# A hybrid decoder layer on one core: rows of the mixed activations and of h loaded in larger pieces into other buffers, and one PSUM bank fewer in rotation

## The chip, the cores and the metric

The kernel runs on one core of a Trainium2 chip. The metric is the device time of one execution, in microseconds (us); the time before is the median of three executions, 2020.22 us (2017.64 to 2026.35). A profiled execution is a further one, taken with the hardware profiler. The engines are named as in the profile: PE (matrix products; PEld its weight loads), ACT (activations and copies), DVE (elementwise), POOL (elementwise, slower), SP (here used to issue DMAs). SPq and ACTq are the DMA issues of SP and ACT.

## The reference

One layer over 2048 tokens of width 1024, all in float32:

```python
hn = rms_norm(h, mix_pre_g)
proj = hn @ w_in                                  # q, k, v and the conv group's input u
attn_out = sliding_window_attention(q, k, v, attn_sinks, rel_bias)
conv_out = conformer_conv(u, conv_dw, conv_dw_b, conv_ln_g, conv_ln_b, w_conv_pw)
mixed = jnp.concatenate([attn_out, conv_out], axis=-1) @ w_out
h = h + rms_norm(mixed, mix_post_g)
hn = rms_norm(h, ffn_pre_g)
ff = (jax.nn.silu(hn @ w_gate) * (hn @ w_up)) @ w_down
h = h + rms_norm(ff, ffn_post_g)
```

The attention has 8 heads of width 64 and a window of 128; the convolution group is a GLU, a causal depthwise convolution of 31 taps, a layer norm, a swish and a 512 by 512 product. The feed-forward width is 2816.

## The kernel before, in words

**Numbers.** Every float32 operand of a product is split into a high and a low part (a copy by ACT, then a subtraction by DVE or POOL), and each product is three matmuls, high by high, high by low, low by high. A split operand is a tile `hl(tag)` of 128 partitions by 2 by 512. The tokens are cut into four blocks of T = 512; the channels into eight blocks (c or k) of 128.

**Stages**, by the label that the names in the profile carry after the @:

- A0 to A3: the input projection of the four token blocks. Its last four channel blocks are the queries.
- B0 to B3: attention. Each of four sub-blocks writes its 128 tokens into `mixT[0:4]`, a DRAM buffer of eight channel blocks by 2048 tokens, from a tile `at` (L517 to L522).
- C0 to C3: the convolution. The taps run on DVE beside the products of other stages (L554). The tail (L568) turns the sums in the PSUM bank `ct` into a tile `yt`, takes the norm, turns them back and writes `mixT[4:8]` (L607).
- U: the pointwise product and the lower half of `w_out` are multiplied once into `fold`.
- W0 to W3: the output projection of the four token blocks (`stage_w`, L693), with its norm (`norm_w`, L745), which writes h into `h_scr` and the normed h into `hn_scr`.
- H0, H2: the operands of the feed-forward for the first pair of token blocks (0 and 1) and the second (2 and 3). `stage_h_plain` (L822) loads columns of `hn_scr`, turns four 128 by 128 pieces on PE, has ACT copy them out scaled (L828), sends that to `hT` and splits it. `stage_h_sums` (L835) forms sums and differences from `hT` and the other block's columns, two blocks of channels at a step, four steps, three tiles `chl` each.
- F0, F2: gate and up products of a pair, in a scheme that needs seven products where eight would be plain (`STEPS`, L867). A part is computed early (`stage_pre`, L880) and kept in DRAM (`keeps`); the rest is `stage_p1` (L950).
- G0, G2: the down projection of a pair, again seven types of products (`stage_p2`, L1108). `finish` (L1086) norms the result, loads rows of h from `h_scr`, adds them and writes `out`. In G0 it runs four times, with two jobs of 128 rows each: O0.1 and O0.3 after type 5, E0.1 and E0.3 after type 6.

**`stage_w` in more detail.** W0 takes the eight channel blocks in four groups of two, W1 to W3 in two groups of four. For a group, `acts` (L699) loads the rows of `mixT` one channel block at a time into a tile with the tag `mtag` (`fa` for W0, `at` for the others) and splits each into a tile `hl(htags[gi])`. Then, for the two halves n of the output, the weights are loaded and four chains of matmuls follow, one for each 128 tokens. The next group's `acts` is called before the second half (L728). In W1 the second group's `acts` is called in the middle of the eight early products of F0 that stand between the groups (L733 to L738). The chains of W2 and W3 go to the PSUM banks `tr`, and the results to four tiles `mid`.

**Buffers.** A tile is asked for by tag, and each tag has a fixed number of buffers, which its tiles share:

```python
BUFS = dict(x=4, p=4, wx=1, gb=2, hl=8, ql=4, chl=5, mid=4, mb=2, fa=4, at=2, fc=3, glu=2, yt=1, raw=2, w=6)
mm = lambda: bank("mm", 4)
tr = lambda: bank("tr", 3)
ct = lambda: bank("ct", 1)
```

`wx`, `chl` and `raw` hold two blocks of 512 columns, `yt` four. `chl` is used by U, by A1, by the splits of W1 to W3 (second group), by `norm_w` (one tile of gains and four of x), by the sums of H and by the weights of F. `wx` is used at the start, by U, by the sums of `w_down` (`stage_tsums`, L1070) and by the rows of h in G0.

**What sets the order.** The program is traced as one main line of stages (`run`, L1343) and several lanes of side work (`Lane`, L1265), which are pumped by the main line's progress: lane `lw` holds in this order C2, W2, C3, W3, the first half of H2, and W3's norm, and runs beside G0; lane `lf` holds the four calls of `finish`; lane `lh` the sums of H. The context that places the instructions (L1491) lays them out on the engines by a simulated timeline, with the traced order as their priority; each engine then runs its own list in order and waits where data or a buffer isn't there.

Of the kernel before, what the change touches and what calls it, by code (L numbers as in the profile page):

```python
# [12 lines left out]
F32 = mybir.dt.float32  # L13
# [4 lines left out]
AF = mybir.ActivationFunctionType  # L18
ALU = mybir.AluOpType
# [6 lines left out]
P = 128  # L26
T = 512
# [10 lines left out]
def layer_kernel(ctx, tc, x, xT, cols, rows, sinks, relb, onehot, w_in, w_pw, w_out, w_gate, w_up, w_down, out):  # L38
    nc = tc.nc
# [15 lines left out]
    def t_(tag, shape, dt=F32):  # L55
        return sb.tile(list(shape), dt, tag=tag, name=nm(tag), bufs=BUFS[tag])

    def f4(tag, shape=(P, D)):
        return t_(tag, shape)

    def f2(tag, shape=(P, T)):
        return t_(tag, shape)

    def hl(tag):
        return t_(tag, (P, 2, T), F32R)
# [624 lines left out]
                vtt(acc[i][:, cs], acc[i][:, cs], o, ALU.add)  # L690
            yield 0.65 * len(units)

    def stage_w(w, atag, htags, mtag, bank_of, norm=None, ready=None):  # L693
        G = KC // len(htags)
        L = f"W{w}"
        lab[0] = L
        acc = [f4(atag) for _ in range(4)]

        def acts(gi):  # L699
            aa = []  # L700
            lab[0] = L
            for c in range(G * gi, G * gi + G):
                m = f2(mtag)
                nc.sync.dma_start(m, mixT[c, :, w * T : (w + 1) * T])
                a = hl(htags[gi])
                act(a[:, 0], m, AF.Copy)
                vtt(a[:, 1], m, a[:, 0].bitcast(F32), ALU.subtract)
                aa.append([a])
            return aa

        def weights(gi, n):
            ws = []
            for c in range(G * gi, G * gi + G, 2):
                if c < 4:
                    ws += weight(w_out[c : c + 2, :, n * T : (n + 1) * T].rearrange("c p t -> p c t"), lo_out[n, c : c + 2], w > 0, on_pool=False)
                else:
                    for j in range(2):
                        ws.append(hl("w"))
                        nc.sync.dma_start(ws[-1].bitcast(F32), fold[n, c - 4 + j])
            return ws  # L720

        nxt = acts(0)
        yield W_LEAD
        for gi in range(KC // G):
            aa = nxt
            for n in range(2):
                lab[0] = L
                if n == 1 and gi + 1 < KC // G and not (ready and G * gi + G == 4):  # L728
                    nxt = acts(gi + 1)
                ws = weights(gi, n)  # L730
                yield from block_half(acc, list(zip(aa, ws)), n, gi == 0, L, bank_of)
            if ready and G * gi + G == 4:
                for i, c in enumerate(ready()):  # L733
                    if i == Q0 // 2:
                        ld.until("C1")
                        lab[0] = L
                        nxt = acts(gi + 1)
                    yield c  # L738
        tail = norm_w(w, acc)
        if norm:  # L740
            norm(tail)
        else:
            yield from tail
# [60 lines left out]
    def turned(w, k, bank_of, tag):  # L804
        c = load_cols(w, k, tag)
        b = bank_of()
        for s in range(4):
            nc.tensor.transpose(b[:, s * P : (s + 1) * P], c[:, s], ident)
        return b
# [12 lines left out]
    def stage_h_plain(ws, ops, n, off):  # L822
        L = f"H{ws[0]}"
        for k in range(4):
            lab[0] = L
            b = turned(ws[0], k + off, tr if ws[0] else ct, COLTAG[ws[0]][k] if ws[0] else "fa")
            u = f2("gb")
            act(u, b, AF.Copy, scale=g_ffn[:, k + off : k + off + 1])  # L828
            nc.scalar.dma_start(hT[ws[0] // 2][k + off], u)
            o = op_tile(ws, ops, n, k, {})  # L830
            act(o[:, 0], u, AF.Copy)
            lo(u, o, False)
            yield 2.0
# [46 lines left out]
    def stage_pre(ws, ops, mid, keep, q0=0, q1=None):  # L880
        PRE = PRES[ws[0]]
        q1 = q1 or 2 * PRE
        L = f"F{ws[0]}"
        raws = {}
        wops = {}
        kept = {}

        def load(q):
            if q < q1 and q % 2 == 0:
                lab[0] = L  # L890
                half, m = divmod(q, PRE)
                raw = t_("raw", (P, 2, T))
                for j in range(2):
                    src, pr = MATS[m + j]
                    nc.sync.dma_start(raw[:, j], src[2 * pr][:, half * T : (half + 1) * T])
                    raws[q + j] = raw[:, j]

        def fetch(q):
            if PRE <= q < q1:
                lab[0] = L  # L900
                kept[q] = f2("gb")
                nc.sync.dma_start(kept[q], keep[q - PRE])

        def split(q):
            if q < q1:
                lab[0] = L
                raw = raws.pop(q)
                wops[q] = split_f(raw, hl("w"))
                lo(raw, wops[q], ws[0] and q % 2 == 1)

        seeded = {}

        def seed(q):
            if PRE <= q < q1:
                lab[0] = L
                seeded[q] = mm()
                act(seeded[q], kept.pop(q), AF.Copy)  # L917

        load(q0)
        load(q0 + 2)  # L920
        for q in range(q0, q0 + 3):
            split(q)
        for q in range(q0, q1):
            half, m = divmod(q, PRE)
            started.add(f"P{ws[0]}.{q}")
            bn = "B21" if half else "B11"
            if len(ops.get(bn, ())) < 4:
                lh.until(f"{bn}.{ws[0]}")
            split(q + 3)
            load(q + 4)  # L930
            fetch(q + 2)
            lab[0] = L
            seed(q + 1)
            lab[0] = L
            o = seeded.pop(q) if half else mm()
            product(o, wops.pop(q), ops[bn], not half)
            if not half:
                u = f2("fa")
                act(u, o, AF.Copy)
                nc.scalar.dma_start(keep[m], u)  # L940
            else:
                if MATS[m][0] is w_gate:
                    sg = f2("fa")
                    act(sg, o, AF.Silu)
                else:
                    vtt(sg, sg, o, ALU.mult)
                    nc.sync.dma_start(mid[0, MATS[m][1]], sg)
            yield 2.76
# [137 lines left out]
    def finish(L, gb, jobs, pool=True):  # L1086
        lab[0] = L
        n_ = len(jobs)
        ssq = sm(4)
        for j, (rows_, halves) in enumerate(jobs):  # L1090
            for n in range(2):
                act(junk[:, 0:T], halves[n], AF.Square, scale=D**-0.5, accum_out=ssq[:, 2 * n + j : 2 * n + j + 1])
                (ptt if pool or n else vtt)(halves[n], halves[n], gb[n], ALU.mult)
            yield 2.0
            lab[0] = L
        vtt(ssq[:, 0:n_], ssq[:, 0:n_], ssq[:, 2 : 2 + n_], ALU.add)
        r = rsqrt(ssq[:, 0:n_], n_, 1, pool)
        for j, (rows_, halves) in enumerate(jobs):
            ht = f4("wx" if L == "G0" else "mid")
            nc.sync.dma_start(ht, h_scr[rows_])  # L1100
            for n in range(2):
                cs = slice(n * T, (n + 1) * T)
                stt(halves[n], halves[n], r[:, j : j + 1], ht[:, cs], ALU.mult, ALU.add)
                nc.sync.dma_start(out[rows_, cs], halves[n])
            yield 2.0
            lab[0] = L
# [236 lines left out]
    def run(gen):  # L1343
        for c in gen:
            clk[0] += c
            for lane in lanes:
                lane.pump(c)
# [5 lines left out]

    lb.add("X", stage_x(), lambda: "x1" in started)
    lu.add("U", stage_fold(), lambda: "A2" in started)
    lw.add("W0", stage_w(0, "x", ["hl"] * 4, "fa", mm), lambda: "A3" in started and "C0" in ld.done and "U" in lu.done)
    TGA = [["hl"] * 8, ["mid"] * 4 + ["chl"] * 4, ["hl"] * 8, ["mid"] * 4 + ["hl"] * 4]
    xa = {}
    warm = mm()
# [46 lines left out]
    ws, ops = (0, 1), {}  # L1406
    for n, off in (("B11", 0), ("B21", 4)):
        lh.add(n + ".0", stage_h_plain(ws, ops, n, off))
    run(stage_w(1, "mid", ["hl", "chl"], "at", mm, norm=lambda g: lh.add("N1", g), ready=lambda: stage_pre(ws, ops, mids[0], keeps[0], 0, Q0)))
    lc.hold = lambda: "S0" not in lh.done  # L1410
    lh.until("B21.0")
    lh.add("S0", stage_h_sums(ws, ops), lambda: f"P0.{PRE_S0}" in started and "B3" in lb.done)
# [5 lines left out]
    lc.rates["T3"] = RC3  # L1418
    ws, ops = (2, 3), {}
    lw.add("C2", stage_tail(2))  # L1420
    lw.add("W2", stage_w(2, "mid", ["ql", "chl"], "at", tr))
    lw.add("C3", stage_tail(3), lambda: since(lc, "T3", CS))
    lw.add("W3", stage_w(3, "mid", ["ql", "chl"], "at", tr, norm=lambda g: lw.add("N3", g)))
    lw.add("B11.2", stage_h_plain(ws, ops, "B11", 0))
    run(stage_p2((0, 1), mids[0], td))
    lw.until("N3")
# [69 lines left out]
```

## Time and profile before

| | |
|---|---|
| median of three executions | 2020.22 us |
| the profiled execution | 2014.8 us |
| its span, first to last instruction | 2013.1 us |
| PE busy | 1941.8 us, 96% |
| DVE, ACT, POOL busy | 1455.3, 953.1 and 333.8 us |
| mean granted clock of PE | 0.987 |

The span is what the views of the trace divide. "Busy" is the time in which an engine had an instruction; register and semaphore work and DMA issues aren't counted. In a list of waits, each row names the waiting instruction, what it waited for, the total in us, how many times, and the longest. In a timeline, each row is a start in us, a duration, the engine, the line, the operation, output and inputs by tile name, the shape and a count, and in brackets how long the engine had been idle and who released it. In a table by stretches, each row has the stretch, its length, the busy time with the number of instructions, the granted clock, the DMA share and GB/s. In a list of DMA issues, each row has the number of transfers, the size of one in KB and the median time in us from issue to landing.

### The profile page before, as it was taken

Reading aid. Unit: us, or ns where it says so; the run is one execution under the profiler, and the core shown is the slowest. Engines: PE = TensorE matmul, PEld = TensorE weight load, DVE = VectorE, ACT = ScalarE, POOL = GpSimd, SP = SyncE. Lnnn points to the kernel's source line nnn. Section 1 sums busy time; section 2 is a strip of 40 time slices with the busy share of each in tenths; the row PEclk is TensorE's granted clock in tenths of the full one; section 3 lists DMA queues with packets and bytes.
Section 4 is the critical chain, followed back from the end, with each engine's and each line's share of the span. In section 5 each row is a group of like instructions: output and inputs, shape, how many; then the busy total and the mean of one; then the engine's idle time right before and its main releaser. Section 6 shows DMA issues by size and latency. Waiting matters only on the chain.

```text
span 2013.1 us, 26722 instructions
## 1 busy us (share of the span) xinstructions
PE 1941.8 (96%) x8730; PEld 1549.1 (77%) x8730; DVE 1455.3 (72%) x2578; ACT 953.1 (47%) x1878; POOL 333.8 (17%) x415
## 2 busy tenths in 40 slices
PE   8999999999989999899999999899999999999997
PEld 6777767677767877687878877777788888888886
DVE  5999969886865898888759964667566665555557
ACT  5355444436637543333345554754634333345443
POOL 4011111012111200000000020144323332311003
PEclk9999999999999999999999999999999999999999
DMA  8787757668659867885378787877844442366654
GB/s 311 255 305 235 234 175 240 200 189 300 217 191 357 271 219 234 274 270 183 122 255 276 273 277 235 297 236 238 303 170 168 167 152 100 127 221 207 210 193 146
DMA packets 229723, 454.56 MB, mean 226 GB/s; under 512 B 22952, under 2 KB 48720, under 8 KB 229584
## 3 DMA queue, kind: packets, MB, share of 16 engines
q1 hardware_dynamic: 211344, 426.64, 63.1%
q10 hardware_dynamic: 18240, 26.22, 3.5%
q8 instruction: 69, 1.13, 0.2%
q14 instruction: 70, 0.57, 0.1%
HBM read 331.65 MB, written 121.12 MB: 225 GB/s over the span
## 4 chain that ended last, share of the span: by engine, by line
PE 43%; DMA 12%; DVE 7%; issue 3%; POOL 2%; ACT 2%; SPq 1%; ACTq 0%; DVEq 0%; POOLq 0%
PE mm@F L85 26%; PE mm@G L85 13%; PE tr@W L85 3%; DMA gb@F<-keeps 2%; DMA td<-fc@G 1%; DMA mids<-fa@F 1%; DMA wx@G<-h_scr 1%; DMA raw@F<-w_up 1%; DVE hl@G L94 1%; DMA at@W<-mixT 1%; DVE w@F L94 1%; DMA mixT<-fc@C 1%; DVE x@G L94 1%; DVE chl@F L94 1%; DMA chl@H<-hT 1%
## 5 line engine op out<-in xcount | busy, mean ns | idle before, releaser
L94 DVE SCALAR_TENSOR_TENSOR fc@C<-glu@C,colt,fc@C 128x512 f32<-128x512 f32 x480 | 355.3, 758 | 2.6
L85 PE MATMUL mm@F<-hl@H,w@F 128*128 128x512 f32 x1056 | 254.5, 392 | 3.9 <-ACT mm@F L917 2.6
L85 PEld LDWEIGHTS mm@F<-hl@H,w@F 128*128 128x128 f32 x1056 | 198.5, 189 | 46.5 <-ACT mm@F L917 3.5
L85 PE MATMUL mm@G<-hl@G,hl@G 128*128 128x512 f32 x924 | 231.0, 395 | 2.4 <-ACT hl@G L790 1.7
L85 PE MATMUL mm@A<-hl@A,w@A 128*128 128x512 f32 x840 | 208.9, 397 | 5.0 <-ACT w@A L127 1.6
L85 PEld LDWEIGHTS mm@G<-hl@G,hl@G 128*128 128x128 f32 x924 | 173.8, 190 | 40.1 <-ACT hl@G L790 2.5
L85 PE MATMUL mm@G<-w@G,hl@G 128*128 128x512 f32 x876 | 199.4, 389 | 0.0
L85 PEld LDWEIGHTS mm@G<-w@G,hl@G 128*128 128x128 f32 x876 | 164.4, 188 | 34.1
L790 ACT ACTIVATE w@F<-chl@F 128x512 fp32r<-128x512 f32 x220 | 134.9, 624 | 117.5 <-PE mm@F L85 110.9
L85 PEld LDWEIGHTS mm@A<-hl@A,w@A 128*128 128x128 f32 x840 | 156.4, 189 | 43.5 <-issue 2.3
L94 DVE TENSOR_TENSOR w@F<-chl@F,w@F 128x512 fp32r<-128x512 f32 x198 | 143.6, 728 | 41.9 <-ACT w@F L790 41.4
L85 PE MATMUL mm@F<-ql@H,w@F 128*128 128x512 f32 x528 | 132.2, 397 | 15.1 <-ACT w@F L790 6.3
L85 PE MATMUL mm@F<-mid@H,w@F 128*128 128x512 f32 x528 | 131.8, 395 | 1.7 <-ACT mm@F L917 1.7
L85 PE MATMUL mm@F<-p@H,w@F 128*128 128x512 f32 x528 | 131.9, 396 | 0.0
L85 PEld LDWEIGHTS mm@F<-ql@H,w@F 128*128 128x128 f32 x528 | 99.8, 191 | 39.6 <-ACT w@F L790 7.1
L85 PE MATMUL mm@F<-x@H,w@F 128*128 128x512 f32 x528 | 125.3, 390 | 0.0
L85 PEld LDWEIGHTS mm@F<-mid@H,w@F 128*128 128x128 f32 x528 | 99.3, 189 | 24.6 <-ACT mm@F L917 2.6
L85 PEld LDWEIGHTS mm@F<-p@H,w@F 128*128 128x128 f32 x528 | 101.1, 192 | 21.6 <-ACT at@F L1038 0.2
L127 ACT ACTIVATE w@A<-raw@A 128x512 fp32r<-128x512 f32 x110 | 67.3, 626 | 101.4 <-PE mm@A L85 75.1
L85 PEld LDWEIGHTS mm@F<-x@H,w@F 128*128 128x128 f32 x528 | 98.7, 188 | 20.5
L494 POOL TENSOR_SCALAR_AFFINE_SELECT p@B<-p@B 128x512 f32<-128x512 f32 x62 | 52.1, 847 | 360.1 <-ACT p@B L492 358.6
L94 DVE TENSOR_TENSOR w@G<-raw@G,w@G 128x512 fp32r<-128x512 f32 x73 | 52.0, 712 | 67.9 <-ACT w@G L790 67.1
(300 smaller groups left out, 3313.0 us busy)
## 6 DMA issues: line engine op xcount, KB each, us to landing
mids<-fa@F SPq DMA_DIRECT2D x154, 256.0 KB, 2.6
raw@A<-w_in SPq DMA_DIRECT2D x55, 512.0 KB, 4.7
w@A<-lo_in SPq DMA_DIRECT2D x84, 256.0 KB, 3.4
fc@G<-mids SPq DMA_DIRECT2D x77, 256.0 KB, 3.4
fa@G<-mids SPq DMA_DIRECT2D x75, 256.0 KB, 4.4
gb@F<-keeps SPq DMA_DIRECT2D x72, 256.0 KB, 4.2
w@W<-fold SPq DMA_DIRECT2D x32, 512.0 KB, 6.1
chl@F<-w_gate SPq DMA_DIRECT2D x22, 512.0 KB, 4.0
```

What stands on the lines that cost most here:

```text
L85: r = nc.tensor.matmul(*args, **kw)
L94: r = op(*args, **kw)
L127: act(w[:, 0], raw, AF.Copy)
L494: nc.gpsimd.affine_select(out=pg[:, kb].rearrange("p (i q) -> p i q", q=P), in_=pg[:, 1].rearrange("p (i q) -> p i q", q=P), compare_op=AL ...
L790: act(w[:, 0], x, AF.Copy)
```

## The change

`stage_w` gets a list of tags for the loaded rows, one for each group, in place of one tag. A tile with the tag `yt` takes four channel blocks of `mixT` in one DMA (1 MB), one with another tag takes two (512 KB). W0 uses `wx` in place of `fa`; W1 uses `yt` for both groups in place of `at`; W2 and W3 use `chl` for the first group and `yt` for the second in place of `at`. The splits are the same operations on parts of the larger tile.

In `stage_h_plain` the second pair's turned columns go to the bank `ct`, as the first pair's do, in place of the three banks `tr`. In `finish`, the rows of h of G0 go to `chl` in place of `wx`. The number of matmuls, transposes, splits and evacuations does not change; the DMAs of rows of `mixT` go from 32 to 12.

```diff
-    def stage_w(w, atag, htags, mtag, bank_of, norm=None, ready=None):
+    def stage_w(w, atag, htags, rtags, bank_of, norm=None, ready=None):
...
-            for c in range(G * gi, G * gi + G):
-                m = f2(mtag)
-                nc.sync.dma_start(m, mixT[c, :, w * T : (w + 1) * T])
-                a = hl(htags[gi])
-                act(a[:, 0], m, AF.Copy)
-                vtt(a[:, 1], m, a[:, 0].bitcast(F32), ALU.subtract)
-                aa.append([a])
+            n = 4 if rtags[gi] == "yt" else 2
+            for c in range(G * gi, G * gi + G, n):
+                ms = t_(rtags[gi], (P, n, T))
+                nc.sync.dma_start(ms, mixT[c : c + n, :, w * T : (w + 1) * T].rearrange("c p t -> p c t"))
+                for j in range(n):
+                    a = hl(htags[gi])
+                    act(a[:, 0], ms[:, j], AF.Copy)
+                    vtt(a[:, 1], ms[:, j], a[:, 0].bitcast(F32), ALU.subtract)
+                    aa.append([a])
...
-            b = turned(ws[0], k + off, tr if ws[0] else ct, COLTAG[ws[0]][k] if ws[0] else "fa")
+            b = turned(ws[0], k + off, ct, COLTAG[ws[0]][k] if ws[0] else "fa")
...
-            ht = f4("wx" if L == "G0" else "mid")
+            ht = f4("chl" if L == "G0" else "mid")
...
-    lw.add("W0", stage_w(0, "x", ["hl"] * 4, "fa", mm), lambda: "A3" in started and "C0" in ld.done and "U" in lu.done)
+    lw.add("W0", stage_w(0, "x", ["hl"] * 4, ["wx"] * 4, mm), lambda: "A3" in started and "C0" in ld.done and "U" in lu.done)
...
-    run(stage_w(1, "mid", ["hl", "chl"], "at", mm, norm=lambda g: lh.add("N1", g), ready=lambda: stage_pre(ws, ops, mids[0], keeps[0], 0, Q0)))
+    run(stage_w(1, "mid", ["hl", "chl"], ["yt", "yt"], mm, norm=lambda g: lh.add("N1", g), ready=lambda: stage_pre(ws, ops, mids[0], keeps[0], 0, Q0)))
...
-    lw.add("W2", stage_w(2, "mid", ["ql", "chl"], "at", tr))
+    lw.add("W2", stage_w(2, "mid", ["ql", "chl"], ["chl", "yt"], tr))
...
-    lw.add("W3", stage_w(3, "mid", ["ql", "chl"], "at", tr, norm=lambda g: lw.add("N3", g)))
+    lw.add("W3", stage_w(3, "mid", ["ql", "chl"], ["chl", "yt"], tr, norm=lambda g: lw.add("N3", g)))
```

## The prediction

> **What bounds the kernel now.** I read the page first (busy shares, the chain), then who waited for whom on PE, then the tiles that the edits touch, and last the timelines around each PE gap.
>
> ```profile
> span 2013.1 us, 26722 instructions
> PE 1941.8 (96%) x8730; PEld 1549.1 (77%) x8730; DVE 1455.3 (72%) x2578; ACT 953.1 (47%) x1878; POOL 333.8 (17%) x415
> PE 43%; DMA 12%; DVE 7%; issue 3%; POOL 2%; ACT 2%; SPq 1%; ACTq 0%; DVEq 0%; POOLq 0%
> ```
>
> PE is the bound: 2013.1 - 1941.8 = 71.3 us without a matmul is all that this edit, which adds and removes no matmul, can touch. So the sum is one over PE's waits, of which these are in reach (waiting instruction, what it waited for, total us, times, longest):
>
> ```profile
> PE tr@H L808 <- ACT gb@H L828: 5.0, 1, 5.0
> PE mm@W L85 <- ACT chl@W L706: 4.4, 1, 4.4
> PE mm@F L85 <- DVE p@G L1160: 3.0, 1, 3.0
> PE tr@W L85 <- ACT ql@W L706: 2.5, 1, 2.5
> PE tr@W L85 <- ACT chl@W L706: 2.4, 2, 1.2
> PE mm@W L85 <- ACT hl@W L706: 1.4, 2, 1.0
> ```
>
> Behind those at L706 stands `at`, two buffers for everything; behind p@G stands `wx`, one buffer:
>
> ```profile
>   DMA at@W<-mixT: 49.3, 19
>   DMA wx@G<-h_scr: 19.7, 6
> at@W<-mixT SPq DMA_DIRECT2D x24, 256.0 KB, 4.0
> raw@W<-w_out SPq DMA_DIRECT2D x16, 512.0 KB, 5.1
> ```
>
> ACT and DVE sat idle 49.3 us for rows of mixT, DVE 19.7 us for rows of h. Most of that is hidden from PE; the list above is what is not.
>
> **The change part by part.** The profiled execution took 2014.8 us (span 2013.1), 5.4 below the median of 2020.22; I take the sum off the median, since the runs agree no better than that.
>
> (a) *W1, second half (c 4 to 7), `at` to `yt`.* Now the SP queue holds four loads together, and ACT reaches the splits behind the attention's exponentials:
>
> ```profile
> 553.47 15.75 SPq L704 DMA_DIRECT2D at@W<-mixT  x4
> 564.52 1.14 ACT L706 ACTIVATE chl@W<-at@W 128x512 fp32r<-128x512 f32 x2
> 565.19 3.78 PE L85 MATMUL mm@W<-w@W,chl@W 128*128 128x512 f32 x8 [4.38 <-ACT chl@W L706]
> 484.09 0.32 SPq L607 DMA_DIRECT2D mixT<-fc@C  x1
> ```
>
> The last row that is needed was sent out at 484, and ACT had no idle time ahead of 564.52. `at` is shared with the attention blocks still running, `yt` is not: one load can go some 50 us earlier and the splits run in idle ACT time. That loads do move forward as soon as their buffer is free is seen at `wx` under (c). Gain 4.4 (ends 0 and 4.4; I take the whole because the data is 70 us old by then). Three of four issues leave SP as well, and with them the 15.75 us block in front of the next weights.
>
> (b) *W2, first half, `at` to `chl` by twos.* `chl` is free when the last weights of the seven-product stage are split; `at` is still used by that stage and by the first loads of G. The 2.5 us wait goes (ends 0 and 2.5, whole taken).
>
> (c) *Rows of h for the first pair's last stage, `wx` to `chl`.*
>
> ```profile
> L1083 SPq DMA_DIRECT2D td<-wx@G x22: 319/326/440, 296.5 to 887.5; - x22
> L1100 SPq DMA_DIRECT2D wx@G<-h_scr x8: 320/356/747, 891.9 to 1405.3; - x8
> 1361.00:1420.00 59.00, 54.82 (x229) 0.97 0.80 270
> 1358.74 0.75 DVE L94 SCALAR_TENSOR_TENSOR p@G<-p@G,sm@G,wx@G 128x512 f32<-128x512 f32 x1 [3.61 <-DMA wx@G<-h_scr]
> 1360.80 29.57 PE L85 MATMUL mm@F<-ql@H,w@F 128*128 128x512 f32 x122 [3.04 <-DVE p@G L1160]
> 1411.77 0.75 DVE L94 SCALAR_TENSOR_TENSOR x@G<-x@G,sm@G,wx@G 128x512 f32<-128x512 f32 x1 [6.20 <-DMA wx@G<-h_scr]
> ```
>
> The first h row was fetched at 891.9, right after the tile before it in `wx` let go at 887.5, and kept the buffer 450 us: buffers of a tag go out strictly in program order, and as early as they come free. The other seven then load one by one with DVE standing still, and the copy that frees PE's bank queues behind them. Five buffers end that: 3.0 us at 1360.8, and part of the 4.2 that PE idles from 1361 to 1420 (59.00 - 54.82). I take 3.0 and half of 4.2, 5.1 (ends 0 and 7.2). What is late next there is the kept products' loads.
>
> (d) *Second pair's turned columns in the one bank `ct` instead of three `tr`.* Eight groups of four transposes, the same evacuations.
>
> ```profile
> L808 PE MATMUL ct@H<-ident,fa@H x32: 270/272/273, 505.5 to 544.5; 128*128 128x128 f32 x32
> L828 ACT ACTIVATE gb@H<-tr@H,colt x8: 665/669/676, 1270.8 to 1310.2; 128x512 f32<-128x512 f32 x8
> 1290.57 1.12 PE L808 MATMUL tr@H<-ident,at@H 128*128 128x128 f32 x4 [4.97 <-ACT gb@H L828]
> ```
>
> The first pair does this in `ct` already, and no wait of PE for that bank is in the list; the second pair in three banks has one of 5.0, because three groups were placed back to back and the fourth found ACT five us behind. With one bank each group stands after its evacuation in the plan, so lag is paid once or not at all. Ends: all 5.0 won, or seven groups each wait one evacuation, 7 x 0.669 = 4.7 lost. The nearest row is the first pair's, without a wait, but ACT there was less loaded; I take 2.5 won. [...]
>
> (e) *W0, `fa` to `wx` by twos.* The longer wait for hl@W, 1.0, is W0's first. A pair's load is longer than one row's, but needs no slot of the projections' `fa`. Zero taken, ends -1 and +1 by that wait. The single `wx` is refilled after each pair is split, with half a group of matmuls (24) still ahead.
>
> (f) *Four rows in one load (W1 first half, W1, W2 and W3 second halves).* A quarter no longer starts by itself. From 4.0 and 5.1 us, 1.1 per further 256 KB, I estimate 7.3 us for 1 MB, 3.3 after a single row. At W1's second half this is hidden (a). Elsewhere the last row is the one that ends it:
>
> ```profile
> 1236.30 0.38 SPq L607 DMA_DIRECT2D mixT<-fc@C  x1
> 1241.34 0.32 SPq L704 DMA_DIRECT2D at@W<-mixT  x1
> 1245.71 2.34 PE L85 MATMUL tr@W<-w@W,chl@W 128*128 128x512 f32 x9 [1.23 <-ACT chl@W L706]
> 480.42 0.60 PE L601 MATMUL ct@C<-ident,yt@C 128*128 128x128 f32 x4
> 488.70 0.51 PE L85 MATMUL mm@W<-w@W,hl@W 128*128 128x512 f32 x1
> ```
>
> In W3 the load starts at 1241 as now, lands near 1249, and four splits follow. In W1's first half `yt` belongs to the convolution tail until 481, so the rows land near 488.5, are split by 490, and PE, which came to W1 at 488.7, waits one or two us. Three places, 0 to 3.3 each (mm@G lies beside two of them), half taken: -5.0; the 2.4 that PE waits for chl@W today is inside that, +2.4. Net -2.6. [...]
>
> (g) *W3, first half, `chl` by twos.* These now queue behind the five `chl` tiles of W2's norm:
>
> ```profile
> 1175.20 0.33 ACTq L781 DMA_DIRECT2D hn_scr<-chl@W  x1
> 1179.86 5.07 PE L85 MATMUL tr@W<-w@W,ql@W 128*128 128x512 f32 x14 [3.44 <-ACT mid@W L688]
> 1161.64 14.78 PE L85 MATMUL mm@G<-hl@G,hl@G 128*128 128x512 f32 x64
> hn_scr<-chl@W ACTq DMA_DIRECT2D x16, 512.0 KB, 4.3
> ```
>
> 1175.2 + 4.3 + 5.1 and 1.3 for a split (one operation on ACT and one on DVE, 0.6 to 0.7 each as at 564.52 and 1454.04) is 1186: W3 begins 6 us after the place where it waits now, and what it could do before that place goes behind it. mm@G covers that, as the 64 in a row before 1176 do; without that cover it costs 6. I take 0, and leave the 3.4 where it is. Nothing that PE needs waits for W3's end before the sums of the second pair, over 100 us on (1322.7 in the next fence).
>
> Sum: 4.4 + 2.5 + 5.1 + 2.5 - 2.6 = 11.9. 2020.2 - 11.9 = 2008.3, **2008**.
>
> **The rivals.** *Given back (within 0.5%).* The places overlap with other waits: if (c) is worth only its 3.0 and (f) its whole 9.9, 4.4 + 2.5 + 3.0 + 2.5 + 2.4 - 9.9 = 4.9, 2015. If each group in the one bank waits, 11.9 - 2.5 - 4.7 = 4.7, 2015 to 2016 as well; this one has a chance of 0.1. [...] For it: DMA already has 12% of the chain. Against: the gaps at 560 and 1360 have one cause each.
>
> *Slower: the order of `chl`.* The eight rows of h now stand in `chl` before the twelve tiles of the second pair's sums, and the next stage's weights stand behind those.
>
> ```profile
> L849 ACT ACTIVATE chl@H<-tr@H,colt x4: 671/677/689, 1322.7 to 1443.8; 128x512 f32<-128x512 f32 x4
> 1436.50 0.67 ACT L849 ACTIVATE chl@H<-tr@H,colt 128x512 f32<-128x512 f32 x1
> 1452.28 1.74 POOL L794 TENSOR_TENSOR mb@H<-chl@H,mb@H 128x512 fp32r<-128x512 f32 x1
> 1454.04 0.69 DVE L94 TENSOR_TENSOR chl@F<-chl@F 128x512 f32<-128x512 f32 x1 [0.57 <-POOL mb@H L794]
> 1460.20 2.12 PE L85 MATMUL mm@F<-hl@H,w@F 128*128 128x512 f32 x8 [1.26 <-DVE fa@F L94]
> ```
>
> The first of four steps of sums came at 1322.7 and the last two run from 1436.5 to 1454.0, 8.8 us a step; the weights of the next stage follow at once, and PE's first product with the sums waits for them. Behind the h rows, whose last is used at 1411.8, all four steps run late. Begun at 1413 they take 35 us, until 1448: no loss. Begun at 1436.5, where the third began today, they take until 1471.7, and PE stands 17.7 us with nothing else to do. With the 4.9 of the case above that is 2020.2 - 4.9 + 17.7 = 2033. It decides if the last POOL operation on the sums comes after 1455. Against it: with `chl` the h rows come without waits, so the last group should end before 1411.
>
> *The change does not do what it says*: the plan, made from a model of the loads, may be laid out anew from 300 us on, and put waits at places unknown to this trace. Either sign, and it is in all three chances.
>
> **How the numbers follow.** About 0.5%, 10 us, is what the runs (2017.64 to 2026.35) can tell from no change. Faster by more, as summed: 0.41. Within: 0.31 (given back). Slower: 0.28, where the ring of `chl` holds about half and a worse order the rest. The likeliest case's own range is 1998 to 2010: all gains at their ends, 4.4 + 2.5 + 7.2 + 5.0 + 2.4 + 1 = 22.5, give 1998. The whole range runs from there to just over the slower rival's 2033, and leaves out a tenth on each side.
>
> **What would show it.** (a) no wait of mm@W for chl@W near 560 and its four splits before 550; (b) no wait for ql@W; (c) DVE's idle time for rows of h under 5 us and no p@G wait over 1; (d) waits of PE for gb@H under 3 in all; (f) loads of 1 MB landing in about 7.3 us. Wrong would be: PE idle over 71 us in all, a wait over 5 us for yt, or the first product that needs the sums waiting longer than today's 1.3.

## The result, and the profile after

The changed kernel takes 1988.39 us (median of four runs, 1984.14 to 1990.51), the kernel before 2023.28 beside it (four runs, 2017.64 to 2028.99): ratio 0.9835, 95% interval 0.9813 to 0.9857. That is 33 us faster by the ratio (35 by the medians) where 12 were forecast, and below the range's lower end of 1998. The profiled execution took 1988.67 us, at its median; that of the kernel before, 2014.8, lies 8.5 below the median of 2023.28. So the two traces differ by less than the medians: 26.5 us of span. What the other 8 us consist of is in no trace.

The head of the page of the changed kernel (span, busy times, chain by engine), and the list of PE's waits. Its lines from 708 on stand two further down than before.

```profile
span 1986.6 us, 26669 instructions
PE 1930.2 (97%) x8730; PEld 1542.3 (78%) x8730; DVE 1460.2 (73%) x2578; ACT 955.2 (48%) x1878; POOL 336.4 (17%) x415
PE 43%; DMA 10%; DVE 9%; issue 3%; POOL 2%; ACT 2%; SPq 1%; DVEq 0%; ACTq 0%; POOLq 0%
```

```profile
PE mm@G L85 <- ACT hl@G L792: 7.7, 3, 6.5
PE tr@B L85 <- DVE sm@B L454: 5.6, 1, 5.6
PE mm@F L85 <- ACT mm@F L1026: 5.0, 2, 3.8
PE mm@F L85 <- ACT w@F L792: 4.0, 1, 4.0
```

All six waits that the prediction listed as in reach are gone, for gb@H, chl@W, p@G, ql@W and hl@W, and so is the one for mid@W, which it left in place. Time without a matmul fell from 71.3 to 1986.6 - 1930.2 = 56.4 us: 14.9 less. That this is near the forecast of 11.9 is in part luck: the seven waits that went were 22.1 us long, and on balance others took some 7 us back, the first two rows above most of all. The other 11.6 us are in the second row of the head: the same 8730 matmuls kept PE busy for 1930.2 us, where they took 1941.8. No edit touches a matmul. The granted clock tells where this came from. In the view by stretches the busy times stand in the order PE, PEld, DVE, ACT, POOL. Of the kernel before, around the waits for chl@W, mid@W, gb@H and p@G:

```profile
552.00:576.00 24.00, 17.90 (x80) 10.54 (x81) 16.18 (x42) 8.84 (x27) 4.72 (x6) 0.86 0.57 196
1172.00:1190.00 18.00, 14.56 (x58) 11.55 (x57) 7.85 (x13) 13.52 (x22) 1.66 (x5) 0.91 0.84 286
1280.00:1300.00 20.00, 15.03 (x62) 12.25 (x62) 19.58 (x33) 12.57 (x25) 2.91 (x1) 0.83 1.00 365
1352.00:1368.00 16.00, 12.25 (x46) 9.28 (x46) 8.31 (x11) 4.72 (x11) 3.27 (x3) 0.89 0.62 212
```

Of the changed kernel, the place where mm@W no longer waits, that where h rows used to stop DVE, and that of its longest wait:

```profile
556.00:572.00 16.00, 16.00 (x82) 11.53 (x80) 6.50 (x28) 5.35 (x21) 1.29 (x2) 1.00 0.32 109
1346.00:1400.00 54.00, 54.00 (x241) 44.62 (x240) 32.51 (x56) 32.00 (x63) 23.08 (x18) 1.00 0.80 265
1300.00:1330.00 30.00, 23.47 (x97) 18.31 (x96) 22.81 (x35) 16.77 (x38) 18.96 (x26) 0.83 0.90 302
```

A clock of 0.86 over 24 us is 6.8 us at half speed (0.14 x 24 x 2): the wait of 4.4 us for chl@W has 6.8 us behind it in which matmuls start every 0.43 us and not every 0.23. The trace's records of the clock, apart from the run's last 12 us, read:

```
before: half clock from 33.7, 562.8 (6.8), 655.0, 791.5, 822.2, 852.9, 1040.7, 1180.6, 1289.9 (6.8), 1361.5   (3.4 us each unless given), 41.0 us in all
after:  half clock from 487.9 (6.8), 815.6, 877.0, 1314.0 (10.2), 23.9 us in all
```

Inside these stretches PE was busy for 37.6 us with 90 matmuls before, and for 15.6 us with 45 after. A matmul adds 0.22 us to the busy time (1930.2 us for all 8730 in the changed kernel), so half clock cost 17.8 us before and 5.7 after. The difference, 12 us, is the 11.6 of the busy time.

ACT's own waits between 960 and 1400 us, where W2 and W3 run, show another thing that moved: the first two rows are of the kernel before, the last two of the changed one.

```profile
ACT chl@W L706 <- DMA at@W<-mixT: 23.0, 8, 5.9
ACT ql@W L706 <- DMA at@W<-mixT: 19.1, 8, 5.1
```

```profile
ACT chl@W L708 <- DMA yt@W<-mixT: 5.0, 2, 3.5
ACT ql@W L708 <- DMA chl@W<-mixT: 0.9, 1, 0.9
```

ACT stood 42.1 us for rows of mixT, and now stands 5.9. But ACT does not stand less for loads in all. Summed over every row of these lists that names a DMA it is 81.9 us before and 82.1 after, above all since the operands of G now hold it for 46.0 us and not 17.0. The longest of these rows after:

```profile
ACT hl@G L792 <- DMA mb@G<-w_down: 14.9, 4, 10.2
ACT hl@G L792 <- DMA mb@G<-td: 13.8, 9, 3.9
ACT hl@G L792 <- DMA fa@G<-mids: 11.1, 7, 5.9
```

ACT's work is nearly the same in both kernels (953.1 and 955.2 us busy), so its idle time in a stage can shrink only by about what the stage shrinks.

The longest wait of PE in the changed kernel stands behind such a stop. The profile puts it down to a row of h, which the operation that ended it does not read, so what ACT truly waited for stays open:

```profile
1315.38 0.63 ACT L1094 ACTIVATE junk<-p@G 128x512 bf16<-128x512 f32 x1 [5.92 <-DMA chl@G<-h_scr]
1318.33 8.49 PE L85 MATMUL mm@G<-hl@G,hl@G 128*128 128x512 f32 x24 [6.50 <-ACT hl@G L792]
```

### The profile page after: what moved, and what is told of

It reads as the page before. It is cut to its first block, busy times and chain, and to the rows that moved or that the text cites. A ratio compares the mean times of both kernels' runs of the same rounds, so it can differ in the third digit from the quotient of the medians.

```text
span 1986.6 us, 26669 instructions
## 1 busy us (share of the span) xinstructions
PE 1930.2 (97%) x8730; PEld 1542.3 (78%) x8730; DVE 1460.2 (73%) x2578; ACT 955.2 (48%) x1878; POOL 336.4 (17%) x415
## 4 chain that ended last, share of the span: by engine, by line
PE 43%; DMA 10%; DVE 9%; issue 3%; POOL 2%; ACT 2%; SPq 1%; DVEq 0%; ACTq 0%; POOLq 0%
PE mm@F L85 29%; PE mm@G L85 12%; DVE fc@C L94 2%; PE tr@W L85 2%; DMA gb@F<-keeps 1%; DVE hl@G L94 1%; DMA mids<-fa@F 1%; DMA fa@G<-mids 1%; DMA td<-fc@G 1%; DVE w@F L94 1%; DMA fc@G<-w_down 1%; DMA wx@G<-w_down 1%; DVE fa@F L94 1%; DVE chl@F L94 1%; DMA mixT<-fc@C 1%
## 5 line engine op out<-in xcount | busy, mean ns | idle before, releaser
L494 POOL TENSOR_SCALAR_AFFINE_SELECT p@B<-p@B 128x512 f32<-128x512 f32 x62 | 57.6, 938 | 374.0 <-ACT p@B L492 372.7
```

What stands on the lines that cost most here:

```text
L494: nc.gpsimd.affine_select(out=pg[:, kb].rearrange("p (i q) -> p i q", q=P), in_=pg[:, 1].rearrange("p (i q) -> p i q", q=P), compare_op=AL ...
```

## The experiments

In each, the kernel before ran on the same chip (medians 2019.9 to 2024.6 us); a ratio is to it.

### The parts, each alone

The edits are those of the change, one group of lines at a time; tags not named keep their single rows.

```diff
 e1_w1   stage_w(1, ...)            "at"  ->  ["yt", "yt"]
 e2_w23  stage_w(2 and 3, ...)      "at"  ->  ["chl", "yt"]
 e3_ht   finish, rows of h in G0    "wx"  ->  "chl"
 e4_ct   stage_h_plain, second pair  tr   ->  ct
 e16_w0  stage_w(0, ...)            "fa"  ->  ["wx"] * 4
```

> The kernel before with W1 alone loading its rows by fours into yt. Theory A (a wait of PE of more than about 2.5 us costs its length and, through a stretch of half clock behind it, about half of 3.4 or 6.8 us more): the 4.4 us wait for chl@W at 560 and the 6.8 us of half clock behind it go, 7.8 us won, but the wait of 5.6 us near 485, which the changed kernel shows with 6.8 us of half clock behind it, comes with this part, 9.0 us lost: between 0 and 3 us slower. Theory B (a wait costs its length alone): 4.4 won and 5.6 lost, 1 us slower. Theory C (the plan is laid out anew and no part has a price of its own): any change of up to 15 us, with waits at places far from W1.

> The kernel before with W2 and W3 alone loading into chl and yt. Theory A: the waits for ql@W (2.5), mid@W (3.4) and chl@W (2.4) go, with two stretches of half clock of 3.4 us: 8.3 + 3.4 = 11.7 us faster. Theory B: 8.3 us faster. Prediction on record: 2.5 won, 2.6 lost, no change. Theory C: the sum does not follow the waits of W2 and W3.

> The kernel before with the rows of h of G0 alone in chl. Theory A: the 3.0 us wait for p@G and the 3.4 us of half clock behind it go, and some of the 4.2 us idle up to 1420: 4.7 to 8.9 us faster. Theory B: 3.0 to 7.2 us faster. Theory C: other waits move.

> The kernel before with the second pair's turned columns alone in the one bank ct. Theory A: the 5.0 us wait for gb@H and the 6.8 us of half clock behind it go: 8.4 us faster. Theory B: 5.0 us faster. Prediction on record: 2.5 us faster. [...]

> Only W0's rows in wx by twos. By the prediction's sum 0, at most 1 us either way: ratio 0.9995 to 1.0005 and with the order's own share 0.997 to 1.003. Rival (the parts do not add up, and W0 carries what is missing to -35): under 0.997.

| part | median us | ratio (95%) | us, measured | us, predicted |
|---|---|---|---|---|
| W1 (a, a third of f) | 2021.82 | 0.9988 (0.9969 to 1.0008) | -2.4 | -2.8 |
| W2, W3 (b, g, the rest of f) | 2002.91 | 0.9900 (0.9885 to 0.9915) | -20 | -1.6 |
| rows of h (c) | 2014.42 | 0.9954 (0.9937 to 0.9972) | -9.3 | -5.1 |
| one bank (d) | 2020.97 | 0.9985 (0.9968 to 1.0002) | -3.0 | -2.5 |
| W0 (e) | 2024.61 | 1.0023 (1.0006 to 1.0041) | +4.7 | 0 |

The measured column is the ratio times 2020. It adds up to -30, the whole change to -33, so nothing large is seen to come from the parts' meeting, though the intervals of the parts, some 3.5 us either way each, leave room for a few us. In the predicted one, each of the three places of (f) counts 1.65. Four of the five are within 5 us of their forecast, though for W1 and the one bank the interval holds 1, so not even the sign is shown, and the theories on W1 (0 to 3 us lost, 1 lost) aren't told apart. W2 and W3 carry what was missed: 20 us are more than either theory of what a wait costs gave for that part's own waits (11.7 and 8.3). That part alone also took away the waits for gb@H and p@G, which the prediction had given to (d) and (c). Between the first product of G0 and the first of F2 it saves 339.6 - 325.1 = 14.5 us: 9.7 of standing still (18.7 to 9.0) and the rest at half clock (13.7 us of it to 3.4). For the rows of h both theories reach into the interval (5.7 to 12.7 us won). For the one bank the interval leaves out the 8.4 of theory A and the 4.7 lost that the prediction had as its other end, and keeps 5.0 and 2.5. In the run with the h rows alone (a trace of the slowest of its four executions, 2021.94 us), DVE's 19.7 us of standing for them are gone and the stretch from F2's start to its first product with the sums takes 89.5 us and not 97.0. In the run with W1 alone the wait of 4.4 is gone, and PE's timeline shows two new stops:

```profile
492.55 0.59 PE L85 MATMUL tr@B<-kz,ql@A 64*128 64x256 f32 x5 [2.02 <-DVE sm@B L454]
494.44 0.80 PE L85 MATMUL tr@B<-kz,ql@A 64*128 64x256 f32 x4 [1.31 <-ACT ql@A L418]
```

They stand near the first load of 1 MB, with the clock at half from 494.2 to 501.0, where the kernel before had neither. So -2.4 agrees with the forecast of -2.8 by luck: the wait of 4.4 and the half clock behind it were won, and these two stops with as much half clock were lost.

### What a stop of PE costs

```diff
+                for _ in range({3: 12, 5: 14, 7: 16, 9: 18, 11: 20, 13: 22, 15: 24, 17: 27, 19: 30}.get(m, 0) if ws[0] and j == 2 else 0):
+                    act(wops[q][:, 0], raws[m][STEPS[i][1]], AF.Copy)
```

> The changed kernel with work on ACT that is needed for nothing: in nine places of the second pair's last stage of products, 12, 14, 16, 18, 20, 22, 24, 27 and 30 further copies of 128x512 (0.62 us each in the trace) stand ahead of a split that PE needs, so that PE stands still nine times, some 1 to 12 us each, with full work before and after. Theory (a wait costs its length and the clock behind it): time runs in windows of 3.41 us; a window in which PE stood 1.9 us or more is followed by a window at half clock, one with 1.6 us or less is not. So stops under 1.6 us are followed by none, stops over 3.8 us always by one window or more, and each such window adds about 1.7 us; the span grows by the sum of the stops and some 1.7 us for each window. Rival (a wait costs its length alone, and the half-clock windows seen in the kernel before had other reasons): the windows at half clock do not stand behind the stops, and the span grows by the sum of the stops, within 3 us.

One execution was measured, the profiled one (2007.72 us). ACT had more slack there than thought, so no stop was longer than 2.6 us. Five of the eleven stops of the stage, by stretches of 7 us, each with one stop in it; at full clock and without a stop 7 us hold 31 matmuls (399 in 90 us in the changed kernel). The stops, in the order of the rows: 1.00, 1.94, 1.24, 1.26 and 2.62 us.

```profile
1506.00:1513.00 7.00, 6.00 (x27) 4.64 (x26) 2.80 (x5) 4.32 (x8) 0.00 (x0) 1.00 0.31 118
1538.00:1545.00 7.00, 5.06 (x15) 3.68 (x15) 2.91 (x5) 6.50 (x12) 0.00 (x0) 0.76 0.31 108
1583.00:1590.00 7.00, 5.76 (x26) 4.45 (x25) 4.41 (x8) 5.25 (x9) 1.10 (x1) 1.00 0.51 168
1692.00:1699.00 7.00, 5.75 (x26) 4.44 (x25) 3.06 (x6) 5.29 (x10) 1.29 (x1) 1.00 0.22 75
1740.00:1747.00 7.00, 4.38 (x13) 3.08 (x12) 2.59 (x4) 2.41 (x4) 0.00 (x0) 0.76 0.23 76
```

A stop of 1.24 us cost five matmuls, or 1.1 us, its length. One of 1.94 us cost 16, or 3.6 us, and one of 2.62 us 18, or 4.1. The stage grew by 18.4 us (329.1 to 347.5). Summed by the distance between the starts of matmuls, 13.5 of it are stops, 3.2 the 16 matmuls at half clock in two windows (1.6 a window), and most of the rest the slower first matmul behind a stop (0.34 us until the next one starts, where 0.23 is usual). Length alone would have given 13.5, which is 4.9 short and not within the rival's 3. The rival is out, although the longest stops that the theory spoke of did not come about.

What a stop brings can be counted in all 18 traces of this study. In every trace the changes of the clock lie within 2 ns of a grid of 3.41 us. Its place differs from run to run: the half-clock stretches begin 3.03 us past a whole number of steps from the span's start in the kernel before, 3.23 in the changed one. For each window of the grid that ran at full clock, from 10 us on, I added up PE's time without a matmul, and looked at the next window:

```
PE idle in the window    windows    next window at half clock
under 0.7 us             about 4400 4
0.7 to 1.6 us            285        5
1.6 to 1.9 us             59        14
1.9 us and more          130        130
```

The run's last 12 us are not among them; there the changed kernel has a window with 1.9 us without a matmul (1972.7 to 1976.1) and the next one still at full clock. By these counts a stop under 1.6 us was nearly always free of half clock (unless a second fell into the same window), one of 1.6 to 1.9 us in about three of four cases. Of the stops of the two kernels, all six over 3.8 us had a half-clock window behind them, as half of such a stop lies in some window of the grid; of the eight between 1.9 and 3.8 us two had none (2.10 and 2.13 us), which I put down to where the grid falls.

### W1's first half back in `at`

```diff
-    run(stage_w(1, "mid", ["hl", "chl"], ["yt", "yt"], mm, ...
+    run(stage_w(1, "mid", ["hl", "chl"], ["at", "yt"], mm, ...
```

> The changed kernel with W1's first half alone back in at by single rows. Theory: the 5.6 us that PE stands at 485.9, while ACT waits for the load of 1 MB (10.1 us until it landed), and the two half-clock windows behind it (2 x 1.7) go: 1988.4 - 5.6 - 3.4, about 1979 to 1981, ratio to the kernel before about 0.978. Rival (a wait costs its length alone): 1983, ratio 0.980. Second rival (the plan moves the wait elsewhere in the stage): 1986 to 1990, ratio 0.983.

1988.97 us, ratio 0.9830 (0.9810 to 0.9849): the second rival. The wait of 5.6 us for sm@B is gone and the part up to F0's first product is 5.5 us shorter (521.9 to 516.4), but the next part, up to G0, is 6.4 longer (491.1 to 497.5), with more waits on ACT and one more half-clock window. So what was won at this place was given back later. Nor does the trace of the changed kernel put the wait of 5.6 us down to the load of 1 MB, as the expectation has it:

```profile
483.66 0.55 DVE L94 TENSOR_SCALAR fc@C<-glu@C,colt 128x512 f32<-128x512 f32 x1 [7.43 <-DMA mixT<-fc@C]
490.69 1.67 ACT L708 ACTIVATE hl@W<-yt@W 128x512 fp32r<-128x512 f32 x3 [4.69 <-DMA yt@W<-mixT]
491.45 0.80 PE L85 MATMUL tr@B<-kz,ql@A 64*128 64x256 f32 x4 [5.59 <-DVE sm@B L454]
```

ACT's stop for the load lies beside PE's, but PE waited for DVE. DVE had stood 7.4 us until the convolution's buffer `fc` was written out to mixT, and then worked without a pause until after 491. The writes that can have held it were sent out at 476.7 or before, ahead of the load at 480.6.

### The buffers, or the size of the loads

```diff
 e7_w23_rows, on top of e2_w23:
-                nc.sync.dma_start(ms, mixT[c : c + n, ...
+                for j in range(n):
+                    nc.sync.dma_start(ms[:, j], mixT[c + j, :, w * T : (w + 1) * T])
 e8_w23_first, in place of e2_w23:
-    ["chl", "yt"]
+    ["chl", "at"]
```

> Only W2 and W3, in chl and yt as in the run before that did both, but with one load for each row into the same buffers (16 loads of 256 KB and not 4 of 512 KB and 4 of 1 MB). Theory (the gain comes from the other buffers, which take ACT's 42 us of standing still for rows out of the stages of W2 and W3): as with the large loads, ratio 0.990, within 0.002. Rival (the gain comes from fewer and larger loads, so fewer issues on SP's queue): ratio 0.996 to 1.000.

> Only W2's and W3's first halves in chl by twos; the second halves stay in at by single rows. Theory (each half's own waits of ACT for rows cost what stands behind them): the wait for ql@W (2.5 and one half-clock window) and that for mid@W (3.4 and one window) go, 9 us; the second half's waits, 2.4 for chl@W, and gb@H's 5.0 with its two windows, stay: ratio 0.995 to 0.997. Rival (the second halves alone carry the gain): 0.999 to 1.001. Second rival (either half is enough): 0.990 to 0.992.

2018.72 us, 0.9982 (0.9966 to 0.9998), and 2017.27 us, 0.9970 (0.9954 to 0.9987). My theory that the buffers alone bring it fell: with one load for each row most of the gain is gone, and the waits for gb@H (5.1) and p@G (2.6) are back. With the first halves alone it is 6 us, at the edge of the theory's range: the waits for ql@W and mid@W are gone as it had them, but that for gb@H, which was to stay at 5.0, is 2.1. So the first halves alone are not enough; the second halves alone were not run. Two timelines of ACT show the difference, of single rows first, then of one load of four:

```profile
1097.86 0.62 ACT L709 ACTIVATE chl@W<-yt@W 128x512 fp32r<-128x512 f32 x1
1098.38 0.62 ACT L793 ACTIVATE hl@G<-mb@G 128x512 fp32r<-128x512 f32 x1
1098.91 0.61 ACT L793 ACTIVATE hl@G<-fa@G 128x512 fp32r<-128x512 f32 x1
1106.22 0.63 ACT L709 ACTIVATE chl@W<-yt@W 128x512 fp32r<-128x512 f32 x1 [6.70 <-DMA yt@W<-mixT]
```

```profile
1097.13 0.63 ACT L792 ACTIVATE hl@G<-mb@G 128x512 fp32r<-128x512 f32 x1 [1.57 <-PE mm@G L85]
1097.67 0.61 ACT L792 ACTIVATE hl@G<-fa@G 128x512 fp32r<-128x512 f32 x1
1102.01 2.20 ACT L708 ACTIVATE chl@W<-yt@W 128x512 fp32r<-128x512 f32 x4 [3.73 <-DMA yt@W<-mixT]
```

With single rows the plan puts the splits of the early rows ahead and that of the last row soon behind them; its load goes out only at 1102.1, and ACT stands 6.7 us at this split, with everything behind it in its list. With one load there is one stop for all four.

### The order that the plan falls into

Since the plan lays the instructions out by its own timeline, an edit of a load moves hundreds of instructions. To see what that alone is worth, one number was nudged, which changes the pace of W2's and W3's lane by less than 1% and no load, buffer or operation:

```diff
-    RC0, RC1, RC2, RC3, RW0, RW, RB, LC = 0.7, 1.1, 0.4, 0.9, 1.7, 1.25, 0.8, 100
+    RC0, RC1, RC2, RC3, RW0, RW, RB, LC = 0.7, 1.1, 0.4, 0.9, 1.7, 1.26, 0.8, 100
```

> The kernel before with nothing of the change: only the pace of the lane that holds C2, W2, C3, W3 goes from 1.25 to 1.26, which does the same work with the same loads and buffers, but has the plan lay the instructions out anew from about 640 us on (179 of 8643 on PE stand elsewhere). Theory A (what was measured for W2 and W3 with large loads, -20 us, is worth of the loads): this kernel is as fast as the kernel before, ratio 0.998 to 1.002. Theory B (the time hangs on the order that the plan falls into, and any small edit moves it by as much): ratio off by more than 0.003 in either direction.

> The same with the pace at 1.24 (288 of 8643 instructions on PE stand elsewhere). Theory A: ratio 0.998 to 1.002. Theory B: off by more than 0.003, and not by the same as with 1.26.

> W2 and W3 in chl and yt with the large loads, and the pace of their lane at 1.26. Theory A: as without the other pace, ratio 0.988 to 0.992, no wait of PE for gb@H or p@G over 2 us. Theory B: it lies elsewhere, anywhere from 0.985 to 1.0, and waits for gb@H or p@G can be back.

> W2 and W3 in chl and yt with one load for each row, and the pace of their lane at 1.26. Theory A: as without the other pace, ratio 0.996 to 1.0. Theory B: it lies elsewhere, and can be as low as the 0.990 of the large loads.

> The whole change with the pace of W2's and W3's lane at 1.26 and not 1.25. Theory (the part of W2 and W3 is worth some 20 us in any order, and the order that the plan falls into adds or takes up to 6): 1980 to 1994, ratio 0.980 to 0.986; ACT's idle time for rows of mixT in W2 and W3 stays under 10 us. Rival (the 35 us are a lucky order): 1995 to 2010, ratio 0.987 to 0.994, nearer to the predicted 2008.

> The whole change with that pace at 1.24. Theory: ratio 0.980 to 0.986. Rival (a lucky order): 0.987 to 0.994.

> W2 and W3 in chl and yt with one load for each row, the pace of their lane at 1.24: the third order of this form. Theory (the buffers alone are worth some 9 us, the large loads some 13 more, as ACT's idle time for rows, 42, 18 and 8 us, has it; the order adds or takes up to 6): ratio 0.992 to 0.998. Rival (the number of loads makes no difference, and the first order with single rows was an unlucky one): 0.987 to 0.991.

| kernel | pace 1.25 | 1.26 | 1.24 | ACT idle for rows of mixT in W2 and W3, us |
|---|---|---|---|---|
| before | 1 | 1.0022 (1.0006 to 1.0038) | 0.9995 (0.9977 to 1.0012) | 42.1, 44.5, 36.5 |
| W2, W3, single rows | 0.9982 | 0.9926 (0.9897 to 0.9956) | 0.9959 (0.9940 to 0.9978) | 18.6, 19.6, 12.9 |
| W2, W3, large loads | 0.9900 | 0.9878 (0.9855 to 0.9902) | | 8.2, 6.8 |
| the whole change | 0.9835 | 0.9831 (0.9807 to 0.9854) | 0.9845 (0.9819 to 0.9871) | 5.9, 4.7, 13.8 |

Both theories hold in part. In the kernel before, the pace moves the time by 0.0022 at most, about as A has it. With large loads A holds but for 0.0002, and no wait for gb@H or p@G is over 2 us. With single rows B holds (0.9926 where A had 0.996 or more). The whole change and the last run with single rows came as their theories had it, and their rivals are out. The order alone moves a kernel by up to 11 us (single rows, 0.9982 to 0.9926), and single waits come and go with it. PE's waits between 960 and 1400 us in the kernel before with the pace at 1.24 begin with

```profile
PE mm@G L85 <- ACT hl@G L790: 7.9, 3, 4.5
PE mm@F L85 <- ACT fa@F L939: 3.7, 2, 3.1
```

and have none for gb@H or mid@W, though its time is that of the kernel before. But the values of the four rows of the table do not overlap, though some of their intervals do. At the same pace the buffers are worth 4, 19 and 7 us (mean 10), and the large loads 17 and 10 us more; there is no run with large loads at 1.24. The whole change stays at 0.983 to 0.985 in three orders, and no lucky order explains it. ACT's idle time for the rows falls from row to row of the table along with the time, though not within a row (13.8 us at 0.9845). ACT's idle time for all DMAs between 960 and 1400 us shows no such steps: by rows of the table it is 78 to 82, 76 to 85, 71 to 77 and 66 to 82 us. That the large loads bring their share was shown by changing nothing else. How they do it is not shown: fewer stops for rows is one account, and another order of ACT's list, which such an edit also brings, is the other.

## Why the prediction was off

The direction was right, and most of the waits that were to go did go; the size failed in two steps.

**"71.3 us without a matmul is all that this edit [...] can touch" and "So the sum is one over PE's waits", each at its length.** Of the 26.5 us by which the traces differ, 11.6 are time with a matmul. The seven waits that went (the six listed and the one for mid@W) had half-clock windows behind them, two each behind the 4.4 and the 5.0, one each behind 3.4, 3.0 and 2.5: seven windows at 1.6 us, or 11 us, on the lengths. That this is also the 11.6 us of the whole trace is in part a coincidence: of the other five windows of the kernel before three are gone as well, and five new ones stand behind the waits for sm@B and hl@G, with PE idle in 8.2 us of them. It was to be had from the rows that the prediction quoted: its own row for 1361 to 1420 has a clock of 0.97, and the 4.2 us that it took from it as idle left this out. In the counts of all 18 traces, 1.9 of 3.41 us without a matmul was enough for a half-clock window in all 130 cases (a run's last 12 us left out).

**(b), (f) and (g), W2 and W3 for 1.6 us together.** The prediction read "ACT and DVE sat idle 49.3 us for rows of mixT", called most of it hidden from PE, and then priced the edits on the waits that name ql@W and chl@W. Measured: 20 us, with the waits for gb@H, p@G and mid@W gone too, 9.7 us less standing of PE in that stage, and 13.7 us of half clock down to 3.4. (f) has the wrong sign there: "a quarter no longer starts by itself" was entered as a cost of up to 3.3 us a place, and with single rows in the same buffers the kernel is 17 and 10 us slower. Why those three waits went is open. An idle ACT in front of a row held up what stood behind in its list (the 6.7 us above), but it is not shown that they were late ends of such stops. With large loads W3's last rows are split at 1246.0, no sooner than before (1245.0), and DVE still stands 14.1 us for rows of h, yet the waits for gb@H and p@G are gone. The kernel before at pace 1.24 has 36.5 us of stops for rows and no wait for gb@H. The landing was taken well enough: 1 MB landed in 5.1 to 10.1 us with a median of 5.8, where 7.3 was estimated.

Point by point, by the signs that the prediction named:

- (a) As forecast at its place. W1's second half is split at 504.0 to 506.1, and mm@W runs at 560.17 without a gap. In W1's first half the load landed after 10.1 us. Beside it PE waited 5.6 and not "one or two us", with two windows at half clock behind it, but for DVE and not for the load.
- (b), (g) No wait for ql@W or mid@W. W3's rows did not queue behind W2's norm until 1175: their loads went out at 1141.3 and 1153.2. W3's first product came at 1147.5, 10 us later than before (1137.1) and not at 1186, and at no cost: PE has no wait for a tile of W there, and the last product of this group came at 1202.9 and not 1218.2.
- (c) DVE's idle time for rows of h went from 19.7 us to none, and no wait for p@G is left. 9.3 (5.7 to 12.7) against 5.1, with the upper end at 7.2. The half-clock window behind the wait would add 1.6; whether the clock is the whole of the difference is not shown.
- (d) No wait for gb@H, and alone 3.6 us of it in two waits against 5.0. The price of one bank, 4.7, was not paid: ratio 0.9985 (0.9968 to 1.0002). That -3.0 is close to -2.5 shows little, as the waits for p@G (5.4) and mid@W (4.6) are longer in that trace than before.
- (e) +4.7 alone, where 0 was taken. That is within what the order moves by itself, so it is open whether it belongs to W0's loads; the rival, under 0.997, is out.

The rivals: "given back" describes W1 alone, not the change. The ring of `chl` did not close:

```profile
1424.54 1.74 POOL L796 TENSOR_TENSOR mb@H<-chl@H,mb@H 128x512 fp32r<-128x512 f32 x1
1432.77 3.56 PE L85 MATMUL mm@F<-hl@H,w@F 128*128 128x512 f32 x15
```

The last POOL operation on the sums ended at 1426.3, 28 us sooner than before and well under the 1455 of the rival, and the first product with the sums came without a wait. So it did before: the first was at 1457.85, and the row at 1460.20 with its 1.26 us, which the prediction took for it, is a later one that waited for DVE's work on `fa`. That the plan may be laid out anew was named, but only as a rival; it should have stood in the range as some 10 us either way.

## What to carry to other kernels

Price a stop of PE by its length and by the clock behind it: in the view by stretches a granted clock under 1.00 beside a wait is part of that wait's price (here stops of 1.94 and 2.62 us cost 3.6 and 4.1). A sum of an engine's idle time neither prices an edit nor names its cause: 36 of ACT's 42 us for rows went here, and it stood as long for other loads. Before calling such time hidden, look at what stands behind it in that engine's list. Where a scheduler lays out the whole program, nudge a number that means nothing and measure, before a few us are given to an edit.

## What the runs showed of the hardware that was not expected

In the 18 traces the granted clock changed only on a grid of 3.41 us. Apart from a run's last 12 us, with 1.9 us or more without a matmul in a window of it the next ran at half clock in 130 of 130 cases, with 0.7 to 1.6 us in 5 of 285. A stop of 1.94 us cost about 1.9 times its length (3.6 us), and stops of 1.24 and 1.26 us cost no more than theirs (1.1 us each).

Four of the 18 traces have a half-clock window that begins at 386.5 to 389.9 us, with no gap of PE in the window ahead of it (W0's part, beside A3); they are the four in the first row of the table of windows. In that window PE starts only 9 or 10 matmuls, one by one in two shapes, where some 15 start elsewhere, and its busy time there is modelled. Whether that is the cause is open.
